# The RWKV recurrence of a three-mixer block: per-chunk state matrices in closed form, on quarters of the TensorE array

## The chip, the cores and the metric

The kernel runs on one core of one Trainium2 chip. The metric is the device time of one execution in microseconds; the kernel before takes 1756.44 us, the median of 3 runs (1751.82 to 1756.74). All views below are of one profiled execution.

## The reference

One layer of a trunk of 512 tokens and width 1024, in float32: an RMS norm, one input projection for three token mixers (RWKV-7, HGRN2, Mamba-2) and their gates, a gated sum of the three, an output projection, then a SwiGLU block of width 2816 and a final norm. The change is in the RWKV-7 mixer alone, 16 heads of width 64. Cut to its core, it computes for each head, token by token,

```
def step(state, inp):
    r_t, w_t, k_t, v_t, ka_t, kb_t = inp
    sa = jnp.einsum('bhvk,bhk->bhv', state, ka_t)
    state = (state * w_t[:, :, None, :] + sa[..., None] * kb_t[:, :, None, :]
             + v_t[..., None] * k_t[:, :, None, :])
    return state, jnp.einsum('bhvk,bhk->bhv', state, r_t)

xs = ... (r, jnp.exp(log_w), k, v, -kk, kk * a)
_, o = lax.scan(step, state0, xs)
```

followed by a norm of o over each head, a bonus term, and a gate. The state is 64x64 a head, and the recurrence runs over all 512 tokens.

## The kernel before

The two heads of a pair lie on partitions 0 to 63 and 64 to 127; there are eight pairs. The 512 tokens are cut into 8 chunks of 64. Three functions do a pair:

- `r_stage1` projects k, r and v with dense matmuls, forms the decays, the decayed queries AR (two blocks of 64 a chunk: A for the state's own correction, R for the output) and keys BK (B and K), then the masked score matrices of each chunk, SB and KAo (128 stationary columns, 64 rows, 128 moving columns, one matmul a head and chunk), and the transposes of BK and v, which give BKt and UV. UV holds, per chunk and head, the state on one half of the partitions and v on the other.
- `r_inverse` inverts the triangular part of the scores of all chunks (VectorE, and two trips through DRAM) and writes it into SB.
- `r_chain` walks through the 8 chunks in order. For each chunk: a matmul of [A scores; A] with UV (tile rw), copied to rb by ScalarE; the output's first part (tile ru, from UV); the inverse times rb (ru<-rb,SB), copied by VectorE over v in UV and by ScalarE to ub; the state's update (ru<-UV,BKt), which VectorE joins with the decayed old state (tile sx, decay WL) and writes as the state of the next chunk; the output's second part (ru<-ub,SB), copied to Ot by ScalarE. So every chunk waits for the one before it. Norm, transposes of Ot, gate and store follow.

All these small matmuls are plain f32, which the hardware runs as two passes, so each of them stands twice in the trace. The dense projections are split in a high and a low part of a faster type, three matmuls each (names hh, hl with wh, wl and the like), of 128x128 stationary and 512 or 256 moving columns.

The order of all instructions is worked out ahead of time: a recorder takes every operation with its operands, and `flush` lists them by simulated readiness and by a priority (`nc.prio`). The chain and the inverse of a pair have priority 0, stage 1 of the next pair 1, HGRN2 2, Mamba-2 3 and up; so the dense work of later stages fills TensorE's queue between the steps of a chain. TensorE takes its queue in that order. The planner's cost of a matmul is in `passes`; before, it knows one array with one end time (`self.pe`), and gives 0.02 us to a small f32 matmul whose output begins at a partition other than 0.

PSUM tiles that matter here are the single banks rd (`psk`), rs (`pss`), rw (`psr`) and ru (`psu`). Every instruction goes through one helper, so all rows carry its line L392 and are told apart by the names of tiles.

Of the kernel before, what the change touches and what calls it, by code (L numbers as in the profile page):

```python
# [14 lines left out]
AF = mybir.ActivationFunctionType  # L15
# [69 lines left out]
class Recorder:  # L85
# [6 lines left out]
    def __init__(self, tc):  # L92
# [13 lines left out]
        self.pe = (0.0, 0.0)  # L106
# [93 lines left out]
    def passes(self, out, method, args):  # L200

        n = 1
        for d in out.shape[1:]:
            n *= d
        load = args[1].shape[-1] / 1200
        if method == "transpose" or args[1].dtype == F32R:
            return load, [n / (1200 if method == "transpose" else 2226)]
        if out.offset & 0xffffff and self.region(out)[1]:
            return load, [0.02]
        return load, [n / 1200] * 2  # L210
# [31 lines left out]
    def add(self, eng, method, args, kw):  # L242
# [44 lines left out]
        for ap in wr:  # L287
# [5 lines left out]
              self.shares(eng, method, args, kw, out)]  # L293
# [4 lines left out]
    def flush(self):  # L298
# [33 lines left out]
        while left > len(order):  # L332
# [27 lines left out]
            if e == "tensor":  # L360
                load, ps = op[9]
                loaded, end = self.pe
                loaded = max(loaded, ready[k])
                for d in ps:
                    loaded = max(loaded + load, end + 0.003)
                    end = loaded + d
                self.pe = (loaded, end)
                op[4] = end - t
            t = max(t, ready[k])
            if e != "gate" and op[10]:  # L370
# [30 lines left out]
class Kern:  # L401
# [46 lines left out]
    def load_consts(self, rk):  # L448
# [6 lines left out]
        nc.sync.dma_start(out=self.m4, in_=self.cdram[:, C_M4:C_M4 + 4])  # L455
        self.one = self.t(self.mx, [P, 1], "one")
# [314 lines left out]

    def r_stage1(self, rk, p):
# [64 lines left out]

        bk = t([P, 8, 2, 64], "BK")
        halves = (slice(0, 64), slice(64, 128))
# [8 lines left out]
        for i, hs in enumerate(halves):  # L848
            nc.vector.tensor_tensor(out=bk[hs, :, 1 - i, :], in0=v3(a)[hs], in1=v3(Ei)[hs], op=ALU.mult)
# [12 lines left out]
        kao = t([P, 8, 128], "KAo", 2)  # L862
        nc.scalar.copy(out=kao[64:128], in_=arf[64:128])
        ka = (arf, kao)
# [24 lines left out]
        for g in range(2):  # L889
            pt = self.pss([P, 4, 2, 64])  # L890
            for c in range(4):
                nc.tensor.transpose(pt[:, c].rearrange("p h v -> p (h v)"), bkf[:, g * 4 + c, :], self.ident)
            nc.scalar.copy(out=bkt[:, :, g * 4:g * 4 + 4, :].rearrange("p h c v -> p c h v"), in_=pt)

        UV = t([P, 8, 2, 64], "UV", 2)
        pv = self.pss([P, 4, 2, 64])
        for c in range(NT):
            nc.tensor.transpose(pv[:, c].rearrange("p h v -> p (h v)"), v[:, c * P:(c + 1) * P], self.ident)
        for hh in range(2):
            hs = slice(hh * 64, hh * 64 + 64)  # L900
            ks = slice(64 - hh * 64, 128 - hh * 64)
            u4 = UV[:, :, hh, :].rearrange("p (c two) v -> p c two v", two=2)
            nc.scalar.copy(out=u4[ks, :, 0, :], in_=pv[0:64, :, hh, :])
            nc.scalar.copy(out=u4[ks, :, 1, :], in_=pv[64:128, :, hh, :])
            nc.gpsimd.memset(UV[hs, 0, hh, :], 0.0)
        return dict(WL=WL, KA=ka, SB=sb, BKt=bkt, UV=UV, bv=bv, dP=dP, dQ=dQ, p=p)

# [62 lines left out]
    def r_chain(self, rk, c_):  # L970
        nc = self.nc
        t = lambda shape, tag, bufs=1, dt=F32: self.t(rk, shape, tag, dt, bufs)
        KA, SB, UV, BKt, WL, p = c_["KA"], c_["SB"], c_["UV"], c_["BKt"], c_["WL"], c_["p"]
# [12 lines left out]
        Ot = t([P, 4, 2, 64], "Ot")  # L986
        sx = t([P, 64], "sx")
        H = (slice(0, 64), slice(64, 128))
        for c in range(8):
            RB, UB = self.rb, self.ub  # L990
            bw = self.psr([P, 2, 64])
            for hh in range(2):
                nc.tensor.matmul(bw[0:64, hh, :], KA[hh][:, c, 0:64], UV[:, c, hh, :],
                                 start=(hh == 0), stop=(hh == 1), skip_group_check=True)
            bu = self.psu([P, 4, 64])
            for hh in range(2):
                nc.tensor.matmul(bu[64:128, hh, :], KA[hh][:, c, 64:128], UV[:, c, hh, :],
                                 start=(hh == 0), stop=False, skip_group_check=True)
# [627 lines left out]
```

## Time and profile before

| | |
|---|---|
| median of 3 runs | 1756.44 us |
| the profiled execution | 1759.52 us |
| its span, first to last instruction | 1757.7 us |
| mean granted TensorE clock | 0.978 |
| TensorE matmul busy | 1702.4 us (97%), 10382 instructions |
| VectorE busy | 1092.3 us (62%), 2622 |
| ScalarE busy | 927.3 us (53%), 1843 |
| GpSimd busy | 261.2 us (15%), 295 |
| DMA engines' mean share | 38% |

A matmul's time in a row is from its start to its modelled end; matmuls overlap, so the distance between starts tells what each one takes. The RWKV pairs run from about 95 to 845 us, with HGRN2 and part of the Mamba-2 work between their steps. In the rows, `d`, `g`, `rd`, `m` and so on are PSUM tiles that are written, and the names behind the arrow are moving and stationary operands; 128*64 is rows by columns of the stationary operand, 128x512 partitions by moving columns.

### The profile page before, as it was taken

The page shows a single profiled execution, that of the slowest core. Times are in us where ns is not written, and L with a number is a line of the kernel's source. Part 1 is how long each engine was busy: PE and PEld are TensorE (multiplying, and loading weights), DVE is VectorE, ACT ScalarE, POOL GpSimd, SP SyncE. Part 2 cuts the span into 40 slices and gives each one's busy share as a digit, 9 for nine tenths or more (in the row PEclk, how much of TensorE's full clock was granted, in tenths as well). Part 3 has the DMA queues.
Part 4 walks back from the last instruction along what each step waited for, and adds up shares of the span by engine and source line. Part 5 has one row for each costly group of instructions (what it writes and reads, how often), then busy time and mean ns, then how long its engine had stood idle before and what let it go on. Part 6 is the DMA issues. An engine that isn't in the chain of part 4 may idle for free. (4 is left out here: it accounts for less than half of the span.)

```text
span 1757.7 us, 29033 instructions
## 1 busy us (share of the span) xinstructions
PE 1702.4 (97%) x10382; PEld 1328.1 (76%) x10382; DVE 1092.3 (62%) x2622; ACT 927.3 (53%) x1843; POOL 261.2 (15%) x295
## 2 busy tenths in 40 slices
PE   7999999999999999989999999999999999999998
PEld 6786777667676867665878978976788888888886
DVE  5778888687776888885575777554354533333233
ACT  6567665675665566665674668443343533333222
POOL 1112213131221212120120231121111000000000
PEclk9999999899997999998999999999999999999999
DMA  5242323323332233333343445377764333333222
GB/s 162 67 108 72 82 71 90 82 64 88 79 96 64 68 86 84 88 87 82 88 120 93 121 149 173 115 238 236 233 204 148 90 93 93 97 94 92 96 97 78
DMA packets 291311, 191.89 MB, mean 109 GB/s; under 512 B 59053, under 2 KB 255047, under 8 KB 291167
## 3 DMA queue, kind: packets, MB, share of 16 engines
q1 hardware_dynamic: 291167, 190.04, 37.8%
q8 instruction: 82, 1.34, 0.3%
q14 instruction: 62, 0.51, 0.1%
HBM read 164.22 MB, written 25.76 MB: 108 GB/s over the span
## 5 line engine op out<-in xcount | busy, mean ns | idle before, releaser
L392 DVE TENSOR_TENSOR wl<-wr,wh 128x512 fp32r<-128x512 f32 x267 | 187.0, 702 | 251.7 <-ACT wh L392 248.3
L392 ACT CAST wh<-wr 128x512 fp32r<-128x512 f32 x267 | 164.8, 619 | 316.4 <-PE d L392 87.4
L392 ACT CAST rgh<-rgr 128x512 fp32r<-128x512 f32 x142 | 87.8, 618 | 184.2 <-PE rd L392 84.4
L392 DVE TENSOR_TENSOR rgl<-rgr,rgh 128x512 fp32r<-128x512 f32 x142 | 100.7, 710 | 115.6 <-ACT rgh L392 112.1
L392 PE MATMUL d<-hh,wh 128*128 128x512 f32 (+1 forms) x368 | 153.8, 418 | 4.4 <-DVE q L392 3.1
L389 ACT ACT_TABLE_LOAD x121 | 155.2, 1283 | 2.1
L392 PE MATMUL d<-hl,wh 128*128 128x512 f32 (+1 forms) x368 | 152.2, 414 | 0.0
L392 PE MATMUL d<-hh,wl 128*128 128x512 f32 (+1 forms) x368 | 151.0, 410 | 0.7 <-DVE wl L392 0.7
L392 PE MATMUL rd<-hh,rgh 128*128 128x512 f32 (+1 forms) x324 | 131.0, 404 | 1.3 <-DVE r L392 0.5
L392 PE MATMUL rd<-hl,rgh 128*128 128x512 f32 (+1 forms) x324 | 128.4, 396 | 0.0
L392 PE MATMUL rd<-hh,rgl 128*128 128x512 f32 (+1 forms) x324 | 128.4, 396 | 0.0
L392 PEld LDWEIGHTS d<-hh,wh 128*128 128x128 f32 x368 | 71.9, 195 | 24.3 <-issue 6.7
L392 PE MATMUL g<-hh,gwh 128*128 128x512 f32 x192 | 82.4, 429 | 2.9 <-ACT gwr L392 1.8
L392 PE MATMUL g<-hh,gwl 128*128 128x512 f32 x192 | 81.0, 422 | 3.3 <-DVE gwl L392 3.2
L392 PEld LDWEIGHTS d<-hh,wl 128*128 128x128 f32 x368 | 71.6, 195 | 15.9 <-issue 2.2
L392 PEld LDWEIGHTS d<-hl,wh 128*128 128x128 f32 x368 | 71.7, 195 | 15.5 <-issue 2.0
L392 PE MATMUL g<-hl,gwh 128*128 128x512 f32 x192 | 80.8, 421 | 0.0
L392 PE MATMUL d<-wh,hh 128*128 128x256 f32 x256 | 74.3, 290 | 2.5 <-ACT q L392 2.3
L392 PEld LDWEIGHTS rd<-hh,rgh 128*128 128x128 f32 x324 | 61.1, 189 | 19.8 <-DVE r L392 2.3
L392 PE MATMUL d<-wl,hh 128*128 128x256 f32 x256 | 74.5, 291 | 0.0
L392 POOL TENSOR_TENSOR X<-X,q 128x256 f32<-128x256 f32 x56 | 52.3, 941 | 143.6 <-ACT X L392 133.2
L392 PE MATMUL d<-wh,hl 128*128 128x256 f32 x256 | 72.9, 285 | 0.0
(1490 smaller groups left out, 4427.1 us busy)
## 6 DMA issues: line engine op xcount, KB each, us to landing
wr<-in_w_in_dram SPq DMA_DIRECT2D x108, 256.0 KB
rgr<-in_w_in_dram SPq DMA_DIRECT2D x88, 256.0 KB
wr<-in_w_branch_dram SPq DMA_DIRECT2D x59, 256.0 KB
wr<-in_w_ffn_in_dram SPq DMA_DIRECT2D x58, 256.0 KB
gwr<-in_w_in_dram SPq DMA_DIRECT2D x96, 128.0 KB
rgr<-in_w_ffn_in_dram SPq DMA_DIRECT2D x30, 256.0 KB
wr<-in_w_ffn_out_dram SPq DMA_DIRECT2D x30, 256.0 KB
gdram<-gwr SPq DMA_DIRECT2D x24, 256.0 KB
```

The source lines that it names most:

```text
L389: self.nc.scalar.preload_act_table_set(ops[-1 - j][7])
L392: getattr(getattr(self.nc, eng), method)(*[self.resolve(x) for x in args], **{k: self.resolve(x) for k, x in kw.items()})
```

## The change

`r_chain` no longer walks the chunks with all their steps. With the state S at the head of a chunk, a chunk's new state is a matrix M times S plus a matrix N, and its output a matrix Q times S plus a local part; M, N, Q and the local part don't depend on S. They are formed for all chunks in batches (`quads` calls over c = 0 to 7), one read from PSUM a batch; then six serial steps S <- M S + N follow, and one batch adds Q S to all outputs. The decay enters M as eye times WL, made by GpSimd into AR's first half.

`quads` multiplies the two heads as two 64x64 matmuls, each on a quarter of the array (`x` = 0: rows and columns of the same half; `x` = 1: crossed halves). Many batches alternate x and the PSUM bank with the chunk's parity.

In `r_stage1`, BK is built at full height instead of in halves, the scores use quads, masked by 4 operations of 128 partitions instead of 8 of 64, and the transposes of A, v, B and K are quads against an identity of 64 (`eye`) instead of 12 transposes of 128x128; KAo's copy and the parts of UV go. The planner models each quarter of the array in 32x32 parts with their own load and end times (`self.pe`, 16 of them), at least 0.006 us between matmul starts, drops the 0.02 us rule, and counts up to 0.11 us between two operations of VectorE or ScalarE on different partitions.

```diff
+    def quads(self, out, st, mv, x=0, start=True):
+        H = (slice(0, 64), slice(64, 128))
+        for i in range(2):
+            self.nc.tensor.matmul(out[H[i ^ x]], st[H[i]], mv[H[i]], start=start, stop=True, skip_group_check=True)

 r_stage1:
-        for i, hs in enumerate(halves):
-            nc.vector.tensor_tensor(out=bk[hs, :, i, :], in0=v3(kk)[hs], in1=v3(ae)[hs], op=ALU.mult)
+        nc.vector.tensor_tensor(out=bk[:, :, 0, :], in0=v3(kk), in1=v3(ae), op=ALU.mult)
...
-        for g in range(2):
-            gs = slice(g * 4, g * 4 + 4)
-            ps = (self.psk([P, 4, 128]), self.pss([P, 4, 128]))
-            for c4 in range(4):
-                c = g * 4 + c4
-                nc.tensor.matmul(ps[1][:, c4, :], bkf[H[1], c, :], ka[1][H[1], c, :], start=True, stop=True)
-                nc.linked(nc.tensor.matmul, ps[0][:, c4, :], bkf[H[0], c, :], ka[0][H[0], c, :], start=True, stop=True)
-            for hh in (1, 0):
-                hs, ks = H[hh], H[1 - hh]
-                nc.vector.tensor_tensor(out=sb[hs, gs, :], in0=ps[hh][hs], in1=mask[hs], op=ALU.mult)
-                nc.vector.tensor_tensor(out=ka[hh][ks, gs, :], in0=ps[hh][ks], in1=mask[ks], op=ALU.mult)
+        for i, dst in enumerate((sb, ks)):
+            ps = (self.psk([P, 4, 128]), self.pss([P, 4, 128]))
+            for c in range(8):
+                self.quads(ps[c % 2][:, c // 2], bk[:, c, i], arf[:, c], c % 2)
+            for x in range(2):
+                nc.vector.tensor_tensor(out=dst[:, x::2, :], in0=ps[x], in1=mask, op=ALU.mult)
...
+        av = t([P, 2, 8, 64], "UV", 2)
+        for dst, src in ((av, (lambda c: ar[:, c, 0], lambda c: v[:, c * 64:c * 64 + 64])),
+                         (bkt, (lambda c: bk[:, c, 0], lambda c: bk[:, c, 1]))):
+            ps = (self.psk([P, 2, 4, 64]), self.pss([P, 2, 4, 64]))
+            for i in range(2):
+                for c in range(8):
+                    self.quads(ps[c % 2][:, i, c // 2], src[i](c), self.eye, c % 2)
+            for x in range(2):
+                nc.scalar.copy(out=dst[:, :, x::2, :], in_=ps[x])
+        nc.gpsimd.tensor_tensor(out=ar[:, :, 0, :], in0=self.eye.unsqueeze(1).broadcast_to([P, 8, 64]),
+                                in1=WL.unsqueeze(2).broadcast_to([P, 8, 64]), op=ALU.mult)

 r_chain, in place of the loop over the chunks:
+        At, V, B, K = AV[:, 0], AV[:, 1], BKt[:, 0], BKt[:, 1]
+        TA, SBo, Ot = SB[:, :, 0:64], SB[:, :, 64:128], t([P, 8, 64], "Ot")
+        b = self.psr([P, 8, 64])
+        for c in range(8):
+            quads(b[:, c], KS[:, c, 0:64], V[:, c])
+        nc.scalar.copy(out=Ot, in_=b)
+        ba, bv = self.psu([P, 8, 64]), self.psr([P, 8, 64])
+        for c in range(1, 8):
+            quads(ba[:, c], TA[:, c], At[:, c])
+        for c in range(8):
+            quads(bv[:, c], TA[:, c], Ot[:, c])
+        nc.vector.tensor_copy(out=TA[:, 1:8], in_=ba[:, 1:8])
+        nc.scalar.copy(out=Ot, in_=bv)
+        b = (self.psu([P, 4, 2, 64]), self.psr([P, 4, 2, 64]))
+        for c in range(1, 8):
+            quads(b[c % 2][:, c // 2, 0], TA[:, c], B[:, c], c % 2)
+            quads(b[c % 2][:, c // 2, 1], TA[:, c], SBo[:, c], c % 2)
+        for x in range(2):
+            s = AR[:, 2 - x::2]
+            nc.vector.tensor_tensor(out=s, in0=b[x][:, 1 - x:4], in1=s, op=ALU.add)
+        b = (self.psu([P, 4, 64]), self.psr([P, 4, 64]))
+        for c in range(7):
+            quads(b[c % 2][:, c // 2], K[:, c], V[:, c], c % 2, c < 2)
+        for c in range(7):
+            quads(b[c % 2][:, c // 2], B[:, c], Ot[:, c], c % 2, False)
+        for x in range(2):
+            nc.scalar.copy(out=At[:, x:7:2], in_=b[x][:, 0:4 - x])
+        b = self.psu([P, 8, 64])
+        for c in range(8):
+            quads(b[:, c], KS[:, c, 64:128], V[:, c], 0, c == 0)
+        for c in range(8):
+            quads(b[:, c], SBo[:, c], Ot[:, c], 0, False)
+        nc.scalar.copy(out=Ot, in_=b)
+        b = self.psr([P, 8, 64])
+        for c in range(1, 7):
+            quads(b[:, c], AR[:, c, 0], At[:, c - 1])
+            nc.vector.tensor_tensor(out=At[:, c], in0=b[:, c], in1=At[:, c], op=ALU.add)
+        b = (self.psu([P, 4, 64]), self.psr([P, 4, 64]))
+        for c in range(1, 8):
+            quads(b[c % 2][:, c // 2], AR[:, c, 1], At[:, c - 1], c % 2)
+        for x in range(2):
+            o = Ot[:, 2 - x::2]
+            nc.vector.tensor_tensor(out=o, in0=b[x][:, 1 - x:4], in1=o, op=ALU.add)
...
-        po = self.pss()
-        for c in range(NT):
-            nc.tensor.transpose(po[:, c * P:(c + 1) * P], Ot[:, c].rearrange("p h v -> p (h v)"), self.ident)
+        po = (self.pss([P, 4, 64]), self.psu([P, 4, 64]))
+        for c in range(8):
+            quads(po[c % 2][:, c // 2], Ot[:, c], self.eye, c % 2)

 the planner (flush):
-                load, ps = op[9]
-                loaded, end = self.pe
-                loaded = max(loaded, ready[k])
+                load, ps, parts = op[9]
+                loaded = max([ready[k]] + [self.pe[i][j][0] for i, j in parts])
+                end = max(self.pe[i][j][1] for i, j in parts)
                 for d in ps:
-                    loaded = max(loaded + load, end + 0.003)
+                    loaded = self.pe_last = max(loaded + load, end + 0.003, self.pe_last + 0.006)
                     end = loaded + d
...
+            if e in ("vector", "scalar"):
+                if self.parts.get(e) not in (None, op[11]) and t - self.free[e] < 0.1:
+                    t = max(t, self.free[e] + 0.11)
+                self.parts[e] = op[11]
```

## Rows read from the trace of the kernel before

**Rows 1.** Windows: stretch, length, busy of PE, PEld, DVE, ACT, POOL, clock, DMA.
```profile
95.00:845.00 750.00, 726.19 (x5515) 526.29 (x5516) 585.62 (x1718) 464.13 (x1029) 144.52 (x161) 0.96 0.31 80
845.00:1757.00 912.00, 897.82 (x4465) 737.39 (x4463) 444.66 (x760) 404.76 (x711) 101.67 (x106) 0.99 0.43 132
1400.00:1500.00 100.00, 100.00 (x430) 80.68 (x429) 36.95 (x55) 32.25 (x54) 0.00 (x0) 1.00 0.34 97
```

**Rows 2.** Waits of TensorE, 95 to 845: waiter, releaser, total us, times, longest.
```profile
PE ru L392 <- DVE UV L392: 1.4, 2, 0.9
```

**Rows 3.** Timeline of TensorE, one chunk of the chain: start us, us, instruction.
```profile
717.38 0.40 PE L392 MATMUL d<-hh,wh 128*128 128x512 f32 x1
717.70 0.34 PE L392 MATMUL ru<-UV,BKt 128*64 128x64 f32 x4
717.97 0.50 PE L392 MATMUL d<-hl,wh 128*128 128x512 f32 x1
718.31 0.40 PE L392 MATMUL d<-hh,wl 128*128 128x512 f32 x1
718.54 0.40 PE L392 MATMUL d<-hh,wh 128*128 128x512 f32 x1
718.87 0.33 PE L392 MATMUL rw<-UV,AR 128*64 128x64 f32 x2
...
719.46 0.40 PE L392 MATMUL ru<-ub,SB 128*64 128x128 f32 x2
...
720.13 0.39 PE L392 MATMUL d<-hh,wl 128*128 128x512 f32 x1
720.36 0.40 PE L392 MATMUL g<-hh,gwh 128*128 128x512 f32 x1
720.69 0.27 PE L392 MATMUL ru<-UV,AR 128*64 128x64 f32 x1
...
721.40 0.40 PE L392 MATMUL g<-hh,gwl 128*128 128x512 f32 x1
```

**Rows 4.** The same timeline, first and last dense start of another chunk.
```profile
141.38 0.40 PE L392 MATMUL d<-hl,wh 128*128 128x512 f32 x1
...
147.28 0.39 PE L392 MATMUL g<-hh,gwh 128*128 128x512 f32 x1
```

**Rows 5.** The same timeline, the scores of four chunks in stage 1.
```profile
78.40 0.39 PE L392 MATMUL d<-hh,wh 128*128 128x512 f32 x1
...
78.94 0.27 PE L392 MATMUL rs<-KAo,BK 64*128 64x128 f32 x1
78.95 0.27 PE L392 MATMUL rd<-AR,BK 64*128 64x128 f32 x1
79.05 0.27 PE L392 MATMUL rs<-KAo,BK 64*128 64x128 f32 x1
...
79.82 0.50 PE L392 MATMUL d<-hl,wh 128*128 128x512 f32 x1
80.16 0.40 PE L392 MATMUL d<-hh,wl 128*128 128x512 f32 x1
```

**Rows 6.** The same timeline, a batch of four transposes and the next dense start.
```profile
87.07 0.60 PE L392 MATMUL rs<-ident,BK 128*128 128x128 f32 x4
87.42 0.48 PE L392 MATMUL g<-hh,gwh 128*128 128x512 f32 x1
```

**Rows 7.** The same timeline, matmuls of HGRN2 in four column groups.
```profile
398.96 0.70 PE L392 MATMUL m<-X 128*32 128x32 f32 x56
399.59 0.50 PE L392 MATMUL d<-hh,wh 128*128 128x512 f32 x1
```

**Rows 8.** Groups of VectorE, 95 to 845: count, busy us, mean ns, idle before.
```profile
L392 DVE SCALAR_TENSOR_TENSOR UV<-sx,WL,ru 64x64 f32<-64x64 f32 x96 | 26.8, 279 | 15.7 <-PE ru L392 13.8
```

**Rows 9.** Windows, around a fall of the granted clock.
```profile
532.40:535.80 3.40, 2.45 (x18) 1.29 (x18) 3.18 (x9) 3.33 (x6) 0.00 (x0) 1.00 0.57 164
535.80:559.70 23.90, 23.67 (x101) 15.52 (x100) 12.63 (x30) 10.38 (x28) 5.72 (x5) 0.50 0.15 36
```

More of the change, by code (lines that the diff above doesn't have):

```diff
@@ L105, in __init__ @@
         self.dma = 0.0
-        self.pe = (0.0, 0.0)
+        self.pe, self.pe_last = [[(0.0, 0.0)] * 4 for _ in range(4)], 0.0
+        self.parts = {}
         self.port = {"vector": 0.0, "gpsimd": 0.0}
@@ L206, in passes @@
         if method == "transpose" or args[1].dtype == F32R:
[L207 to L210, printed above, removed]
+            ps = [n / (1200 if method == "transpose" else 2226)]
+        else:
+            ps = [n / 1200] * 2
+        rows, cols = ((q[1] // 32, -(-q[2] // 32)) for q in (self.region(args[1]), self.region(out)))
+        return load, ps, [(i, j) for i in range(*rows) for j in range(*cols)]
     def shares(self, eng, method, args, kw, out):
@@ L455, in load_consts @@
         nc.sync.dma_start(out=self.m4, in_=self.cdram[:, C_M4:C_M4 + 4])
+        self.eye = self.t(self.mx, [P, 64], "eye")
+        nc.vector.tensor_tensor(out=self.eye, in0=self.ident[:, 0:64], in1=self.ident[:, 64:128], op=ALU.add)
         self.one = self.t(self.mx, [P, 1], "one")
@@ L847, in r_stage1 @@
         nc.vector.scalar_tensor_tensor(out=a, in0=a, scalar=1.0, in1=k, op0=ALU.add, op1=ALU.mult)
-        for i, hs in enumerate(halves):
-            nc.vector.tensor_tensor(out=bk[hs, :, 1 - i, :], in0=v3(a)[hs], in1=v3(Ei)[hs], op=ALU.mult)
+        nc.vector.tensor_tensor(out=bk[:, :, 1, :], in0=v3(a), in1=v3(Ei), op=ALU.mult)
         nc.vector.scalar_tensor_tensor(out=a, in0=r, scalar=self.pc("rwkv_r_k", p), in1=a,
@@ L861, in r_stage1 @@
         arf = ar.rearrange("p c s t -> p c (s t)")
-        kao = t([P, 8, 128], "KAo", 2)
-        nc.scalar.copy(out=kao[64:128], in_=arf[64:128])
-        ka = (arf, kao)
+        ks = t([P, 8, 128], "KAo", 2)
         sb = t([P, 8, 128], "SB", 2)
@@ L888, in r_stage1 @@
         nc.gpsimd.tensor_tensor(out=bkf, in0=bkf, in1=WL.unsqueeze(2).broadcast_to([P, 8, 128]), op=ALU.mult)
[L889 to L896, printed above, removed]
-        for c in range(NT):
[L898 to L906, printed above, removed]
+        av = t([P, 2, 8, 64], "UV", 2)
[9 more added lines that the diff above has]
+                                in1=WL.unsqueeze(2).broadcast_to([P, 8, 64]), op=ALU.mult)
+        return dict(AR=ar, KS=ks, SB=sb, BKt=bkt, AV=av, bv=bv, dP=dP, dQ=dQ, p=p)
     def r_inverse(self, rk, c_):
@@ L972, in r_chain @@
         t = lambda shape, tag, bufs=1, dt=F32: self.t(rk, shape, tag, dt, bufs)
-        KA, SB, UV, BKt, WL, p = c_["KA"], c_["SB"], c_["UV"], c_["BKt"], c_["WL"], c_["p"]
+        AR, KS, SB, BKt, AV, p = (c_[i] for i in ("AR", "KS", "SB", "BKt", "AV", "p"))
         cs = slice(p * P, (p + 1) * P)
@@ L1033, in r_chain @@
+        po = (self.pss([P, 4, 64]), self.psu([P, 4, 64]))
+        for c in range(8):
+            quads(po[c % 2][:, c // 2], Ot[:, c], self.eye, c % 2)
         y = t([P, S], "y")
-        nc.vector.scalar_tensor_tensor(out=y, in0=po, scalar=self.pc("rwkv_gn_w", p), in1=c_["bv"],
-                                       op0=ALU.mult, op1=ALU.add)
+        y3, bv3 = (x.rearrange("p (c t) -> p c t", c=8) for x in (y, c_["bv"]))
+        for x in range(2):
+            nc.vector.scalar_tensor_tensor(out=y3[:, x::2], in0=po[x], scalar=self.pc("rwkv_gn_w", p),
+                                           in1=bv3[:, x::2], op0=ALU.mult, op1=ALU.add)
```

52 lines of the change are left out of this document (8 added, 44 removed).

## The prediction

> **What bounds the kernel now.** I read the busy times by stretch first. From 95 to 845 us, where the eight RWKV pairs run, TensorE is busy 726 of 750 us; behind that, 898 of 912 [rows 1]. Busy time of pipelined matmuls proves little, so the next view is the waits of TensorE in the first stretch: the longest waits for chain results come to 1.4 us in total, in a stretch of 750 [rows 2]. TensorE always has another matmul to issue, and what matters is how much of its time each piece of work takes. Then the timeline of TensorE. Undisturbed dense matmuls with 512 moving columns start every 0.2326 us (430 in 100 us) [rows 1]. Each time small f32 matmuls stand between two dense ones, the gap is longer. I price such an interruption by the time from the dense start ahead of it to the second dense start behind it, less two pitches (0.465 us); so the slow first dense matmul behind it (0.34 us to the next start) is counted.
>
> **The price of the old steps, per pair of heads.** One chunk of the old chain is in [rows 3]. The state update (ru<-UV,BKt): 718.31 - 717.38 - 0.465 = 0.465 us. The new right side with the old output (rw, then ub): 720.13 - 718.54 - 0.465 = 1.125. Output and solve (ru<-UV,AR, KAo and rb): 721.40 - 720.36 - 0.465 = 0.575. Sum 2.17 us. Another chunk took from 141.38 to 147.28, 5.90 us with 13 dense matmuls in it, so 5.90 - 13 x 0.2326 = 2.88 [rows 4]. These are my ends; I take 2.3, near the first, because in the second TensorE stood for UV. Eight chunks, the last without the update: 8 x 2.3 - 0.47 = 17.9 us. The scores: 80.16 - 78.40 - 0.465 = 1.3 per four chunks [rows 5], 2.6 for eight. The three batches of transposes in stage 1 and the one of the output: 0.35 to the next dense start [rows 6] and 0.10 for its slow start, 0.45 each, 1.8. Old total 22.3 us a pair.
>
> **The price of the new steps.** A quads call is two 64x64 matmuls of two passes each. Its passes: 128 columns are one pass per 0.11 us in a half of the array [rows 5], so 64 columns 0.055. Two row halves run at once (rs and rd start 0.01 us apart) [rows 5], and four column groups too: 56 matmuls of 32 columns in 0.63 us, 11 ns each [rows 7]. I take it that both hold together, so that the two matmuls of a call overlap, and calls on alternating banks (c % 2) use the other two quarters. No row shows row and column groups combined; from below the price is the one used here, from above every pass stands alone (a rival). Passes one behind the other, per pair: KS by V 16; TA by At 14; TA by Ot 16; TA by B and by SBo 14 calls on two banks, 16; K by V and B by Ot 16; the local outputs 2 x 16 = 32; six serial steps 12; the carried output 8; the transpose of Ot 8. That is 138 x 0.055 = 7.6 us. The fixed part of an interruption is 0.465 less its two passes, 0.35 us [rows 3]. Order and banks join some batches: I count the first two as one, then TA by Ot, TA by B, the K/B sums, the local outputs, six steps, the carried output, the transpose: 13 x 0.35 = 4.55. Chain 12.15 us. In stage 1 the scores are two groups of 8 passes of 128 columns (1.76), the transposes two groups of 16 passes (1.76), four interruptions 1.4: 4.9, where the old ones cost 3.95. New total 17.05 us.
>
> Saved: 22.3 - 17.05 = 5.25 us a pair, 42 us in eight. The issue of matmuls doesn't bind: four quarters need one per 0.055 / 4 = 14 ns, and [rows 7] has 11.
>
> The Trainium skill, TensorE: Matmul & The Clock Gate, section "Wait — 56ns, not 53.3ns?", says that matmul starts are never closer than about 25 ns, however small the matmul. The 11 ns of [rows 7] disagree for matmuls in different column groups. By the page, the 300 matmuls a pair in batches on two banks would cost 300 x 10.5 ns more, an estimate of 25 us in all; I go by the row.
>
> **What else moves.** Waits: the old chain hands over four or five times a chunk to ScalarE or VectorE and back, about 300 times in all; the new one some 13 times a pair, 104. A waiting quads call holds everything behind it on TensorE, dense matmuls included, so the six steps (quads, add of 128x64 on VectorE, quads) are the dangerous ones; dense work of later stages stands between them, as it does between the old ones. The few us of idle before chain matmuls [rows 2] fall to a third: I take -3 us, with +10 as the other end should the order written beforehand be wrong by 0.2 us at each of the 48 steps. VectorE loses 20 copies and 22 multiply-adds of 0.28 us a pair [rows 8], and as full-height instead of half-height operations 4 of the 8 score maskings and 2 of the 4 BK products; it gains about 5 us of reads from PSUM: by estimate -10 us a pair of its 586 / 8 = 73 [rows 1]. ScalarE loses about 8 us of 58. Neither bounds; they make weights ready earlier. TensorE's idle 24 us there and the gaps between dense groups shrink; I take -10 us, between 0 and -35. The extra product on GpSimd (eye by WL) costs nothing on the path: GpSimd is busy 145 of 750 us [rows 1]; uncovered it would add under 2 us a pair, ahead of the six steps. No DMA is added or moved on SP's queue. The planner's new model of TensorE and the 0.11 us it now counts for a change of partitions change the order everywhere; within +-10 us, taken as nothing.
>
> Sum: -42 - 3 - 10 = -55 us. The profiled execution took 1759.5 us (span 1757.7 and 1.8 around it): 1704.5. The median of the runs shown is 3.1 us lower, so I predict 1701 us.
>
> **Rivals.** (a) The quarters don't overlap. For: every overlapping pair of row halves in the trace writes two banks (rs and rd) [rows 5], while both matmuls of a quads call write one. If they take turns, each batch without alternation doubles (16 + 14 + 16 + 32 + 12 = 90 passes, +4.95 us) and each with it runs two at a time (48 passes, +2.64; scores +1.76; transposes +1.76): 11.1 us a pair, 89 us; 1701 + 89 = 1790. It turns the sign once more than 6.9 of these 11.1 us a pair are paid. Against: the two write different partitions, and column groups share a bank freely [rows 7]. The Trainium skill, TensorEngine Tiling (Array Packing), section "Restrictions and Gotchas", says that different row tiles cannot use the same PSUM bank at the same time; no run here shows it either way, and its time would be this 1790.
>
> (b) Two at a time but never four: only the batches on two banks suffer, 2.64 + 1.76 + 1.76 = 6.2 us a pair, 49 in all: 1750, no change or barely faster.
>
> (c) The clock. Stretches with few dense columns dropped the granted clock: 535.8 to 559.7 ran at 0.50, 1.2 GHz, after TensorE had been busy for 2.45 of 3.40 us, with 18 matmuls [rows 9]; over the 750 us the mean is 0.96 [rows 1], about 30 us lost. If each new chain brings one such stretch, 8 x 12 us = 96 less the 30 there now: 1701 + 66 = 1767. Against: the batches are shorter than the old chain and dense work lies between.
>
> (d) More is gained: half the idle (12), half the clock loss (15), and the dearer old chunk (2.88 for 2.3 in half of them, 18): about 1701 - 40 = 1660.
>
> **How the numbers follow.** Forecast 0.57 (own range 1675 to 1735), (a) 0.09, (b) 0.09, (c) 0.05, (d) 0.20. Under 0.3%, 5 us here, a measurement of this kernel can't tell a change. Faster: forecast, (d) and a third of (b), 0.80. Same: 0.07, nearly all (b). Slower: (a) most of it, and (c), 0.13. The range 1650 to 1745 holds the forecast's and most of (d), and leaves out (a), (c) and much of (b).
>
> **What would show it.** In the new trace: the two matmuls of a quads call start within 0.01 us of each other; KS by V (32 matmuls) takes about 0.9 us (1.8 would be (a)) and TA by B and SBo (56 matmuls) about 0.9 too (1.5 would be (a) or (b)); the chain breaks the dense stream some 13 times a pair, where three times a chunk is 24 now [rows 3]; the busy time of VectorE between 95 us and the end of the last pair some 80 us less; that stretch shorter by about 55 us and the rest behind it as long as now (912 us). Wrong it would be if the stretch shortened and the rest grew, or if TensorE stood for VectorE in the six steps for more than 1 us a pair.

## The result, and the profile after

The changed kernel takes 1691.07 us (median of 4 runs, 1688.76 to 1691.18); the kernel before, run beside it on the same chip, 1754.13 (4 runs, 1746.37 to 1756.74). By the medians it is 63 us faster; the ratio is 0.9662 [0.9627, 0.9697]. The profiled execution took 1688.76 us, 70.8 less than the one of before.

The totals of its page, engine by engine: busy us, share of the span, instructions.

```profile
span 1687.0 us, 34137 instructions
PE 1642.5 (97%) x13358; PEld 1331.5 (79%) x13358; DVE 1024.3 (61%) x2335; ACT 831.5 (49%) x1519; POOL 267.4 (16%) x285
```

TensorE is as full as before and has 2976 more matmuls; VectorE lost 68 us and ScalarE 96. The granted clock (span and mean) is the first difference that does not come from the arithmetic; it was 0.978 over 1757.7 us before:

```profile
core 0: 1687.0 us, clock 0.994
```

The stretches that answer to [rows 1], with the same columns. The last pair's outputs are now transposed at 690 us, not at 850. The last two stretches are explained below.

```profile
95.00:690.00 595.00, 580.59 (x7905) 465.32 (x7903) 472.81 (x1332) 333.02 (x621) 150.96 (x152) 1.00 0.34 84
690.00:1687.00 997.00, 980.44 (x4885) 801.25 (x4884) 485.61 (x842) 437.03 (x788) 100.97 (x106) 0.99 0.44 131
130.40:147.60 17.20, 16.43 (x499) 13.59 (x498) 14.44 (x33) 7.15 (x13) 3.60 (x4) 1.00 0.36 78
136.20:147.60 11.40, 11.07 (x353) 9.38 (x352) 8.99 (x24) 4.31 (x8) 3.48 (x3) 1.00 0.44 96
```

The stretch of the pairs is shorter by 155 us and the rest longer by 85: pairs now end every 77 us instead of every 94, and dense work of the other mixers that stood between them has moved behind them. So the two stretches can't be compared by themselves, only their sum. The waits of TensorE in 95 to 690 for results of the chain's steps (waiter, releaser, total us, times, longest), all that the view lists, come to 3.5 us. The row of [rows 2] is the longest of five such groups; the five come to 4.6 us in 95 to 845.

```profile
PE ru L402 <- DVE AR L402: 1.6, 2, 0.9
PE ru L402 <- ACT UV L402: 1.0, 2, 0.8
PE rw L402 <- DVE UV L402: 0.9, 2, 0.7
```

The timeline of TensorE over one chain (start us, us, instruction, matmuls in the row) answers to [rows 3]. An f32 matmul has one such record for each of its two passes, and by matmul I mean such a record, as the prediction does. KS lies in the tile named KAo, At and V in UV, B and K in BKt. The fence begins with TA by At (28 matmuls) and TA by Ot; then come parts of TA by B and by SBo on two banks, the local outputs (KS by V, then SBo by Ot), and serial steps (`rw<-UV,AR`) with the next pair's scores (`rs<-AR,BK`) between.

```profile
130.14 0.40 PE L402 MATMUL d<-hh,wl 128*128 128x512 f32 x1
...
130.66 1.03 PE L402 MATMUL ru<-UV,SB 64*64 64x64 f32 x28
131.52 0.98 PE L402 MATMUL rw<-Ot,SB 64*64 64x64 f32 x28
...
133.46 0.23 PE L402 MATMUL rw<-BKt,SB 64*64 64x64 f32 x2
133.50 0.22 PE L402 MATMUL ru<-BKt,SB 64*64 64x64 f32 x2
133.51 0.22 PE L402 MATMUL rw<-SB 64*64 64x64 f32 x2
133.56 0.22 PE L402 MATMUL ru<-BKt,SB 64*64 64x64 f32 x2
...
138.67 1.15 PE L402 MATMUL ru<-UV,KAo 64*64 64x64 f32 x32
139.66 1.04 PE L402 MATMUL ru<-Ot,SB 64*64 64x64 f32 x30
...
140.65 0.22 PE L402 MATMUL rw<-UV,AR 64*64 64x64 f32 x1
140.65 0.27 PE L402 MATMUL rs<-AR,BK 64*64 64x128 f32 x1
...
141.27 0.27 PE L402 MATMUL rw<-UV,AR 64*64 64x64 f32 x2
141.28 0.33 PE L402 MATMUL rs<-AR,BK 64*64 64x128 f32 x2
...
147.65 0.50 PE L402 MATMUL d<-hh,wh 128*128 128x512 f32 x1
```

What to see: 28 matmuls from 130.66 to 131.52 are 31 ns each in the mean. The single records behind this row start in twos: the two halves of a quads call 6 to 7 ns apart, the next two 58 ns after them. So the halves overlap in one bank. On two banks four matmuls start every 58 ns, from 133.35 to 134.3 all 56. And from 130.4 to 147.6 no projection runs, at a clock of 1.00; full-array matmuls stand there only at 134.65 and 135.80 (tmpA and tmpB by a matrix of ones, 512 columns, not in the fence), and from 136.2 on there are small ones alone.

Stage 1 of another pair, transposes of A and v (rows named `eye`), then of B and K, as the same view shows them:

```profile
224.08 0.51 PE L402 MATMUL d<-hh,wl 128*128 128x512 f32 x1
224.72 0.68 PE L402 MATMUL rd<-eye,AR 64*64 64x64 f32 x16
225.23 0.63 PE L402 MATMUL rd<-eye,v 64*64 64x64 f32 x16
225.79 0.27 PE L402 MATMUL m<-X 128*32 128x32 f32 x8
225.99 0.68 PE L402 MATMUL rs<-eye,AR 64*64 64x64 f32 x16
226.51 0.63 PE L402 MATMUL rs<-eye,v 64*64 64x64 f32 x16
...
228.63 0.50 PE L402 MATMUL g<-hh,gwh 128*128 128x512 f32 x1
```

Here all 32 matmuls of the bank rd come first and all of rs later, though the program alternates the banks call by call: the order written out beforehand takes what it reckons ready first, and rs comes free later than rd. 32 matmuls from 224.72 to 225.79 are 33.4 ns each, as if the second bank weren't there. Not every batch is split like this. By my count of the whole trace, a matmul on the other bank starts within 20 ns for 52% of the transposes of stage 1, 98% of the transposes of the outputs and 59% of TA by B and SBo, but for 14% of the K/B sums and 7% of the scores.

**Where the 70.7 us of span went.** Two sums, both from the profiled executions. First the clock: (1 - mean clock) x span is 38.7 us before and 10.1 after, a difference of 28.6; this counts the whole span as TensorE's. Second, I went through the timeline of TensorE, took each distance between two dense starts less its undisturbed pitch (doubled where the clock was low), and put it down to the small matmuls between, shared by their expected time where several kinds stand in one gap. In us, all eight pairs:

| | before | after | arithmetic alone (below) |
|---|---|---|---|
| dense matmuls at their pitch | 1284.2 | 1284.2 | 1284.2 |
| chain | 121.8 | 79.8 | 86.6 |
| scores | 32.5 | 29.2 | 29.1 |
| transposes of stage 1 | 15.0 | 39.1 | 38.0 |
| transposes of the outputs | 5.9 | 9.4 | 13.7 |
| other small matmuls | 171.6 | 168.3 | 170.3 |
| nothing between | 67.1 | 47.1 | 56.6 |
| lost by the clock | 38.7 | 10.1 | 18.9 |

The small matmuls of RWKV gave 17.7 us, gaps with nothing between 20, others 3.3, the clock 28.6: 69.6 of 70.7. How one gap is shared among kinds depends on the expected times, so these rows are estimates. A second count needs none: each small matmul gets the time to the next start, and what a dense one takes beyond its pitch goes to the small ones beside it. It gives, before and after, chain 133.0 and 80.2, scores 36.2 and 39.8, transposes of stage 1 15.2 and 29.7, transposes of the outputs 6.6 and 7.7, other small ones 202.9 and 206.6, nothing between 31.4 and 18.1, and 35.8 and 8.3 lost by the clock. Both counts agree on the chain (42 and 53 us less) and on stage 1 (21 and 18 us more); all small matmuls of RWKV together are 18 us less by the one and 34 by the other.

The clock can be checked without a model. In 44 executions of the kernel before, run beside the experiments, the mean granted clock differed from one to the next, from 0.975 (1760 to 1765 us) to 0.996 (1734.23 us); time and clock go together (correlation -0.97, 13.0 us for each 0.01). Six more executions, slow ones by over 1.5% against the fastest beside them, are not counted. The changed kernel's four executions had clocks of 0.994 to 0.997. At that clock the line through the 44 gives the old kernel some 1736 us, an estimate with one execution near it. So of the 63 us between the medians about 45 are there at the same clock, and about 18 go with the clock; the 28.6 belong to one profiled execution of before, at 0.978.

### The profile page after: what moved, and what is told of

It reads as the page before. It is cut to its first block, busy times and chain, and to the rows that moved or that the text cites. A ratio compares the mean times of both kernels' runs of the same rounds, so it can differ in the third digit from the quotient of the medians.

```text
span 1687.0 us, 34137 instructions
## 1 busy us (share of the span) xinstructions
PE 1642.5 (97%) x13358; PEld 1331.5 (79%) x13358; DVE 1024.3 (61%) x2335; ACT 831.5 (49%) x1519; POOL 267.4 (16%) x285
## 4 chain that ended last, share of the span: by engine, by line
PE 79%; DVE 7%; DMA 5%; ACT 5%; issue 2%; SPq 1%; POOL 1%; POOLq 0%; DVEq 0%; ACTq 0%
PE d L402 21%; PE rd L402 17%; PE g L402 11%; PE m L402 8%; PE rw L402 8%; PE rs L402 8%; PE ru L402 7%; DVE X L402 1%; ACT L399 1%; DMA em<-ydram 1%; DMA wr<-in_w_in_dram 1%; SPq L402 1%; DMA gwr<-in_w_in_dram 1%; DMA gdram<-gwr 1%; ACT wh L402 1%
## 5 line engine op out<-in xcount | busy, mean ns | idle before, releaser
L402 PE MATMUL d<-hh,wh 128*128 128x512 f32 (+1 forms) x368 | 148.1, 402 | 1.8 <-DVE q L402 1.2
L402 PE MATMUL d<-hh,wl 128*128 128x512 f32 (+1 forms) x368 | 147.4, 400 | 0.7 <-DVE wl L402 0.7
L402 PE MATMUL d<-hl,wh 128*128 128x512 f32 (+1 forms) x368 | 145.7, 396 | 0.0
L402 PE MATMUL g<-hh,gwh 128*128 128x512 f32 x192 | 79.8, 416 | 4.1 <-ACT gwh L402 2.0
L402 PEld LDWEIGHTS rd<-hh,rgl 128*128 128x128 f32 x324 | 61.3, 189 | 14.8 <-issue 0.7
```

The costliest lines, as they stand in the source:

```text
L402: getattr(getattr(self.nc, eng), method)(*[self.resolve(x) for x in args], **{k: self.resolve(x) for k, x in kw.items()})
```

## The experiments

The first study took the change apart into arithmetic and planner.

**planner_only**: the kernel before with the planner's part of the change.

```diff
-        self.pe = (0.0, 0.0)
+        self.pe, self.pe_last = [[(0.0, 0.0)] * 4 for _ in range(4)], 0.0
+        self.parts = {}
...
-        if out.offset & 0xffffff and self.region(out)[1]:
-            return load, [0.02]
...
+            if e in ("vector", "scalar"):
+                if self.parts.get(e) not in (None, op[11]) and t - self.free[e] < 0.1:
+                    t = max(t, self.free[e] + 0.11)
+                self.parts[e] = op[11]
```

> The arithmetic of before with the planner's new model of TensorE's quarters and of changes of partitions. If all of the gain is the arithmetic's (small matmuls cheaper, fewer waits, a clock that falls less often), the time stays within 10 us of before: 1744 to 1764 us, and the granted clock stays near 0.98. Rival: the new order is part of the gain, most of all of the clock's share; then 15 to 30 us below before, 1725 to 1740, and a clock of 0.99.

Measured: 1781.75 us (1780.31 to 1784.47), ratio to the kernel before 1.0157 [1.0115, 1.0199], slower, which neither expectation had. **math_only**: the change with the planner as before.

```diff
-        self.pe, self.pe_last = [[(0.0, 0.0)] * 4 for _ in range(4)], 0.0
-        self.parts = {}
+        self.pe = (0.0, 0.0)
...
+        if out.offset & 0xffffff and self.region(out)[1]:
+            return load, [0.02]
...
-            if e in ("vector", "scalar"):
-                if self.parts.get(e) not in (None, op[11]) and t - self.free[e] < 0.1:
-                    t = max(t, self.free[e] + 0.11)
-                self.parts[e] = op[11]
```

> The new arithmetic with the planner's old model (one array, 0.02 us for a small f32 matmul that begins at another partition than 0). If the arithmetic carries the gain: within 10 us of 1691. If the new order carries a part: 1705 to 1725.

Measured: 1719.0 us (1716.95 to 1721.03), 0.9798 [0.9754, 0.9842]. So the arithmetic alone gives 35 us (1754.4 by the ratio, less 1719.0), and the planner another 28 on top of it (to 1691), but it costs 28 where the old arithmetic stays. Span and clock of planner_only, then of math_only:

```profile
core 0: 1779.6 us, clock 0.973
```

```profile
core 0: 1717.4 us, clock 0.989
```

By (1 - clock) x span planner_only loses 48 us to the clock and math_only 18.9, where the kernel before loses 38.7 and the changed one 10.1: of each of the planner's two effects about 9 us are the clock, the rest is order at full clock.

**one_diagonal**: the matmuls of all quads use the same two quarters; the banks still alternate.

```diff
-            self.nc.tensor.matmul(out[H[i ^ x]], st[H[i]], mv[H[i]], start=start, stop=True, skip_group_check=True)
+            self.nc.tensor.matmul(out[H[i]], st[H[i]], mv[H[i]], start=start, stop=True, skip_group_check=True)
```

> As the changed kernel, but x is 0 in every quads call, so only the two quarters on the diagonal are used and no batch runs four at a time; banks, copies and counts are the same. If the alternating batches run four at a time as the prediction priced them (2.64 + 1.76 + 1.76 us a pair): +49 us, 1740. If the scores seldom do, because their two banks come free at different times: +25 to +35 us, 1716 to 1726. Rival (b) of the prediction, two at a time at most: no change, 1691 +-5.

Measured: 1711.5 us, 0.9757 [0.9708, 0.9806]: 20 us more than the changed kernel, between no change and the 25 to 35 us for banks that come free at different times; four at a time throughout was priced at 49. The timeline of TensorE in this kernel shows a part of the reason: a batch of transposes that was split by banks costs what it cost in the changed kernel.

```profile
227.33 0.68 PE L402 MATMUL rd<-eye,AR 64*64 64x64 f32 x16
227.85 0.63 PE L402 MATMUL rd<-eye,v 64*64 64x64 f32 x16
228.41 0.27 PE L402 MATMUL m<-X 128*32 128x32 f32 x8
228.61 0.68 PE L402 MATMUL rs<-eye,AR 64*64 64x64 f32 x16
```

**transposes_thrice**: each transpose of stage 1 is done three times over, 2048 more matmul records.

```diff
-            for i in range(2):
+            for i in (0, 1, 0, 1, 0, 1):
                 for c in range(8):
```

> As the changed kernel, with each batch of stage 1's transposes issued three times into the same bank: 64 more calls a pair, 256 more matmuls of 64 columns. If TensorE's time is what bounds the stretch and four quarters run at once: 2 x 1.76 us a pair, +28 us, 1719. At two at a time +56 us, 1747. If TensorE has slack there: less than +10 us.

Measured: 1765.49 us (1761.27 to 1769.96), 1.0074 [1.0047, 1.0101]: 74 us over the changed kernel, 36 ns for each added matmul, more than either expectation. This isn't the price of the matmuls alone. In the two traces the transposes of stage 1, each counted to the next start, take 26.8 us in the changed kernel and 76.2 here: 49.5 us for 2048 more, 24 ns each, between four at a time (14.4) and a split batch (33.4). The other 25 us lie elsewhere, among them longer waits of TensorE in the stretch of the pairs (for Ot and UV 6.5 and 5.9 us, against 1.8 and 0.9 in the changed kernel). So the added matmuls are on the path, and what delays them delays more.

**no_carry**: the six serial steps no longer depend on each other. Left out is the carry of the state over more than one chunk.

```diff
             quads(b[:, c], AR[:, c, 0], At[:, c - 1])
-            nc.vector.tensor_tensor(out=At[:, c], in0=b[:, c], in1=At[:, c], op=ALU.add)
+        nc.vector.tensor_tensor(out=At[:, 1:7], in0=b[:, 1:7], in1=At[:, 1:7], op=ALU.add)
```

> As the changed kernel, but the six serial steps don't wait for each other: all six multiply the uncarried states, and one add of 128x384 follows; it leaves out the carry of the state over more than one chunk. If the steps cost what the prediction gave them (five interruptions more of 0.35 us a pair): -14 us, 1677. If TensorE also stands between them: -20 to -30, 1661 to 1671. If other small matmuls fill the gaps, as the trace suggests (scores of the next pair between the steps): less than 5 us.

Measured: 1697.22 us, 0.9695 [0.9638, 0.9751]. Nothing is won, where five interruptions at the prediction's price would give 14 us. In this kernel's timeline 18 of the 24 matmuls of the steps are one batch, the other six stand among scores. The order changed elsewhere too: the view of waits now lists 4.7 us for KAo, which the changed kernel's doesn't (lines of the timeline and of the waits in 95 to 690). So a small gain from the steps may be hidden by it.

```profile
142.37 0.69 PE L402 MATMUL rw<-UV,AR 64*64 64x64 f32 x18
```

```profile
PE rd L402 <- DVE KAo L402: 4.7, 3, 2.3
```

**no_partition_rule**: the change without the 0.11 us that the planner counts between two operations on different partitions.

```diff
-            if e in ("vector", "scalar"):
-                if self.parts.get(e) not in (None, op[11]) and t - self.free[e] < 0.1:
-                    t = max(t, self.free[e] + 0.11)
-                self.parts[e] = op[11]
```

> As the changed kernel, with the planner's new model of TensorE but without its 0.11 us for a change of partitions on VectorE and ScalarE. If the model of TensorE's quarters is what made the 28 us between the old and the new planner: 1691 +-5. If the rule on partitions made it: 1710 to 1720.

Measured: 1708.14 us (1704.2 to 1711.28), 0.976 [0.972, 0.980]. With the new arithmetic, taking the rule away costs 17 of the planner's 28 us, and the new model of TensorE by itself gives the other 11. (Taken in another order the parts may differ.)

**banks_together**: the planner may begin a batch on two banks only when both are free.

```diff
+    def together(self, aps):
+        ids = [x.offset >> 24 for x in aps]
+        for i in ids:
+            self.open(i)
+            self.acc.setdefault(i, [])
+        return [self.gate[i] for i in ids if i in self.gate]
...
+            self.nc.ops[-1][5].extend(both)
...
             ps = (self.psk([P, 2, 4, 64]), self.pss([P, 2, 4, 64]))
+            both = nc.together(ps)
...
-                    self.quads(ps[c % 2][:, i, c // 2], src[i](c), self.eye, c % 2)
+                    self.quads(ps[c % 2][:, i, c // 2], src[i](c), self.eye, c % 2, both=both)
```

> As the changed kernel, but in each batch on two banks no quads call is listed before both banks are free, so that the batch isn't split into one bank after the other. In the changed kernel's trace split batches take 33.7 ns a matmul and joined ones 17. If that split is what keeps the gain below its price: -10 to -25 us, 1666 to 1681, with nearly all transposes of stage 1 near 17 ns. If waiting for both banks costs as much as it gives: 1691 +-6. Slower than 1697 if the wait delays the next pair's stage 1.

Measured: 1685.29 us (1683.39 to 1689.94), 0.9634 [0.9595, 0.9672]: 6 us under the changed kernel, with intervals that overlap: what was expected if waiting costs as much as it gives. The batches of transposes and the K/B sums did join (a matmul on the other bank within 20 ns for 89% and 86% of them, by the count above), the scores mostly not (31%). This kernel's timeline of TensorE shows the first and the last of 62 matmuls that alternate in this way:

```profile
89.89 0.22 PE L409 MATMUL rd<-eye,BK 64*64 64x64 f32 x1
89.90 0.22 PE L409 MATMUL rs<-eye,BK 64*64 64x64 f32 x1
89.90 0.22 PE L409 MATMUL rd<-eye,BK 64*64 64x64 f32 x1
89.90 0.22 PE L409 MATMUL rs<-eye,BK 64*64 64x64 f32 x1
89.95 0.22 PE L409 MATMUL rd<-eye,BK 64*64 64x64 f32 x1
...
90.77 0.23 PE L409 MATMUL rd<-eye,BK 64*64 64x64 f32 x2
```

62 matmuls in 0.89 us are 14.4 ns each: four quarters at once, at the price that the prediction used. But with the banks held back, TensorE stands for chain results more than before (waits of TensorE, 95 to 690 us, in this kernel; 0.9 us in two waits in the changed one):

```profile
PE rw L409 <- DVE UV L409: 7.4, 16, 1.6
```

The last study asked whether the planner's gain is a better model or a lucky order: **rule_008** and **rule_014** put 0.08 and 0.14 us in the rule's place, **wait_022** an unrelated latency by 0.01 us, **changed_again** nothing, and **rule_old_math** puts the rule alone into the kernel before.

```diff
 rule_008 (rule_014 has 0.14):
-                    t = max(t, self.free[e] + 0.11)
+                    t = max(t, self.free[e] + 0.08)
 wait_022:
-            return 0.21 if e == "tensor" else 0.14
+            return 0.22 if e == "tensor" else 0.14
 rule_old_math, in the kernel before:
+            if e in ("vector", "scalar"):
+                if self.parts.get(e) not in (None, op[11]) and t - self.free[e] < 0.1:
+                    t = max(t, self.free[e] + 0.11)
+                self.parts[e] = op[11]
```

> The changed kernel again, unaltered, as the yardstick for the three that follow: 1691 +-5 us.

> As the changed kernel, with 0.08 instead of 0.11 us in the planner's rule for a change of partitions. If the 17 us between the changed kernel and the one without that rule come from the rule being right (in the trace a VectorE instruction on other partitions starts 31 ns behind the end of the one before it, one on the same 128 partitions 83 ns ahead of it): within 5 us of the changed kernel, since 0.08 is nearly right. If orders that differ a little differ in time by chance: anywhere from 1680 to 1710, without relation to the rule.

> The same with 0.14. Rule right: within 5 us of the changed kernel, or a little above. By chance: anywhere from 1680 to 1710.

> As the changed kernel, with 0.22 instead of 0.21 us in the planner for the way from TensorE to another engine, which says nothing on partitions or quarters. If a good order follows from a good model: within 5 us of the changed kernel. If the order is a matter of chance: off by up to 15 us either way.

> The kernel before with the planner's rule of 0.11 us for a change of partitions, and the old model of TensorE. If the rule makes orders better because it is right: 10 to 20 us below before, 1735 to 1745, and then the new model of TensorE is what costs the old arithmetic the 31 us of planner_only. If it is the rule that harms the old arithmetic, whose chain changes partitions at nearly every step on VectorE and ScalarE: 10 to 30 us above before, 1765 to 1785.

| kernel | us (range) | ratio to before |
|---|---|---|
| changed_again | 1691.87 (1691.38 to 1695.51) | 0.9648 [0.9611, 0.9685] |
| rule_008 | 1692.68 (1688.57 to 1698.17) | 0.9652 [0.9608, 0.9696] |
| rule_014 | 1707.68 (1703.73 to 1709.95) | 0.9734 [0.9696, 0.9772] |
| wait_022 | 1688.32 (1687.55 to 1689.41) | 0.9625 [0.9589, 0.9662] |
| rule_old_math | 1809.9 (1807.29 to 1819.27) | 1.0329 [1.0285, 1.0373] |

Two small nudges, 0.08 and the other latency, moved the time by 4 us or less against changed_again, as expected if the rule is right; 0.14 moved it by 16 us, about as bad as no rule, where a right rule should have kept it within 5 or a little above. So the study leaves open whether the rule's 17 us are a better model or the chance of one order. With the old arithmetic the same rule costs 55 us, more than either expectation. The rule and the new model of TensorE together cost 28 there (planner_only), so it isn't the new model that harms the old arithmetic: it takes back about half. The windows of rule_old_math show where the time went (the stretch of the pairs; then 3.4 us ahead of one fall of the clock, and the stretch at the low level behind it):

```profile
95.00:890.00 795.00, 755.45 (x5493) 543.42 (x5492) 587.54 (x1715) 461.36 (x1026) 144.43 (x163) 0.91 0.30 76
146.50:149.90 3.40, 2.38 (x18) 1.33 (x18) 2.36 (x7) 2.92 (x8) 1.57 (x1) 1.00 0.20 77
149.90:187.40 37.50, 35.78 (x207) 22.44 (x207) 20.78 (x58) 12.29 (x40) 3.28 (x5) 0.50 0.20 47
```

And the waits of TensorE in 95 to 890 us on chain results (the longest was 1.4 us in [rows 2]):

```profile
PE ru L397 <- ACT Ot L397: 6.3, 13, 0.9
PE rw L397 <- DVE UV L397: 5.3, 11, 0.7
PE ru L397 <- DVE UV L397: 4.1, 5, 1.2
```

TensorE stands for the old chain's results more often, the clock fell to 1.2 GHz (0.50) behind such places, and (1 - 0.957) x 1809.7 = 77.8 us are lost by the clock, 39 more than before. The other 13 of the 52 us between the two profiled spans are waits and order at full clock. Why counting a price that the engines do take makes the old order worse is open; the old chain changes partitions at nearly every step of VectorE and ScalarE, so the rule moves most of its chain, but no run isolates that. The rule also counts its price where the trace shows none, between full height and the half that begins at partition 0 (last section).

## Why the prediction was right, and where its terms were off

The forecast was -55 us and the runs of one study differ by -63; in the profiled executions -70.8. The sign, the place (TensorE's own time) and the size hold. The composition doesn't: three terms were off, and the errors partly cancelled. At the same clock the change is worth about 45 us, less than the forecast; the 18 us or so of the clock, which the sum left out, made up for that. So the closeness of the number is in part luck.

**The price of the old and new matmuls (-42 forecast, -18 or -34 by the two counts).** The chain itself came near: forecast 17.9 to 11.4 us a pair (12.15 less the 0.79 of the output's transposes), measured 15.2 or 16.6 to 10.0; so the 2.3 us a chunk was too dear, and rival (d), which priced half of the chunks higher still, was wrong in that part (its three parts also add up to 45, not 40). The step that failed is stage 1: old scores and transposes were forecast at 3.95 us a pair and took 5.9 or 6.4, the new ones at 4.9 and took 8.5 or 8.7. "The scores are two groups of 8 passes" and "the transposes two groups of 16 passes" assumed that calls on two banks interleave throughout. The banks come free at different times, and nearly all batches of scores and about half of the transposes are done bank by bank, for the transposes 33.4 ns a matmul where 14.4 were possible. one_diagonal agrees (without the second diagonal 20 us are lost, not 49), since a split batch loses nothing with it. banks_together joined most batches, though not the scores, and won only 6 us: TensorE then stood 7.4 us for UV, and what the rest went into is open. So the split is shown, but not that it is all of the miss in stage 1.

**The order ("within +-10 us, taken as nothing").** This was the largest miss in kind. The planner's new model is worth -28 us with the new arithmetic and +28 with the old one. The four corners, medians: old with old 1754, old arithmetic with the new planner 1782, new with the old planner 1719, new with new 1691. Neither part has a value of its own here: the arithmetic is worth 35 us under the one planner and 91 under the other. A forecast that adds parts one by one can't see that; the prediction should have kept a wider end for the order.

**The clock (taken as unchanged, half of its loss given back in rival (d)).** 28.6 of the 70.7 us of the profiled pair, and about 18 of the 63 between the medians, go with the clock. The premise of (c), that each new chain brings a fall, is refuted: between 95 and 690 us the changed kernel's clock fell once, for 3.4 us, and in the stretches above it stayed at 1.00, with TensorE busy 16.43 of 17.20 us and, among small matmuls alone, 11.07 of 11.40. In the kernel before it fell six times between 95 and 845 us, 58 us in all. Three of the falls, 41 us, stand behind steps of a chain: [rows 9], and those at 331.0 and 832.7. The windows of before ahead of these two:

```profile
327.60:331.00 3.40, 1.85 (x17) 0.93 (x15) 3.31 (x7) 3.22 (x7) 0.00 (x0) 1.00 0.53 159
829.30:832.70 3.40, 2.20 (x13) 1.25 (x13) 3.12 (x9) 2.90 (x8) 0.00 (x0) 1.00 0.52 156
```

The other three follow waits for Ot (the normed output of a pair, 1.3 us), for a weight (gwr, 1.8) and for q (3.1). So in these rows TensorE stood still ahead of the falls, mostly between old steps, and the lack of dense columns alone went with no fall. That the missing waits are what gave the clock back is the reading of these rows; no run changed the waits alone.

**Waits and relief (-3 and -10 forecast).** The waits listed for chain results fell from 4.6 to 3.5 us, not to a third. Gaps with nothing between fell by 13 or 20 us by the two counts, the 13 of both terms together or somewhat more. VectorE lost 68 us over the span, against about 80 (10 a pair). The six steps were, as far as the runs show, priced too high: no_carry, in which they don't wait, doesn't give back the 14 us of five interruptions, and the +10 end wasn't needed. The timeline shows the next pair's scores and other small matmuls between the steps (140.65 to 141.28 above). The sign against itself that the prediction named, more than 1 us a pair of standing for VectorE in the steps, didn't come: 0.9 us in all pairs.

**The marks.** The two matmuls of a call start 6 to 7 ns apart, within the 0.01 us named; 32 of them from 138.67 to 139.66 take 0.99 us (0.9 forecast, 1.8 for rival (a)); TA by B and SBo, 56 matmuls, about 0.95 us (0.9; 1.5 for (a) or (b)). Both rivals' mechanisms are refuted: two and four at a time both occur. A part of (b)'s price was paid all the same, by the split of banks. The chain breaks the dense stream 5 to 6 times a pair, not 13, by my count, against 27 before: many batches follow one another or have only other small matmuls between. The mark on the stretches was wrong: the one shrank by 155 us and the rest grew by 85, which the prediction had named as a sign against itself. It was no sign against the mechanism: the pairs just ran closer together.

**The two rules.** Rows first: 28 matmuls from 130.66 to 131.52 us, two row halves in one bank, start in twos, 6 to 7 ns apart, with 58 ns from one two to the next; the two write different partitions of the bank. The Trainium skill, TensorEngine Tiling (Array Packing), "Restrictions and Gotchas", says that different row tiles can't access the same PSUM bank at the same time; this trace disagrees where the partitions differ, and the measurement decides. And 62 matmuls in 0.89 us are 14.4 ns from start to start, where the page TensorE: Matmul & The Clock Gate of the Trainium skill, "Wait — 56ns, not 53.3ns?", gives about 25 ns as the least; across quarters of the array this trace goes below it.

**What is still open.** Whether the 17 us with no rule and the 16 us with 0.14 are the model or chance; why the rule harms the old arithmetic; where most of the gain of joined banks went. wait_022 and banks_together are 3 and 6 us under the changed kernel; the intervals of their ratios overlap with its own, and they were not combined.

## What to carry to other kernels

When a written-out order depends on a cost model, a change of the model is a change of the kernel: try model and arithmetic alone and together, since their effects don't add. Where two matmuls shall use the array side by side on two banks, look in the timeline whether they do; a bank that comes free later splits the batch, here at 33.4 ns a matmul instead of 14.4. And sum the granted clock over the span before explaining a difference by matmuls; better still, look for executions of the two kernels at the same clock.

## What the runs showed of the hardware

Two operations one behind the other on VectorE overlap when their first partition is the same and the second doesn't wait for what the first wrote. They don't overlap when the first partition is another one. The timeline of VectorE of the kernel before shows both within 3 us. In the order of the program the first product of BK is on the half from partition 0, the second on the half from partition 64; the products of AR have full height:

```profile
67.46 0.68 DVE L392 SCALAR_TENSOR_TENSOR AR<-kk,E 128x512 f32<-128x512 f32 x1
68.06 0.68 DVE L392 TENSOR_TENSOR BK<-kk,tmpA 64x512 f32<-64x512 f32 x1
68.67 0.68 DVE L392 TENSOR_TENSOR AR<-r,E 128x512 f32<-128x512 f32 x1
69.38 0.69 DVE L392 TENSOR_TENSOR BK<-kk,tmpA 64x512 f32<-64x512 f32 x1
```

Full height and the first half start 0.60 and 0.61 us apart, though each takes 0.68: the next begins 82 and 73 ns before the end of the last. The second half begins 32 ns after it. The maskings of the scores agree: SB behind KAo, both on the half from 0, begins 72 to 76 ns before the end (12 of 12 times); AR on the half from 64 behind SB on the half from 0 begins 13 to 32 ns after it (12 of 12). Two halves one behind the other take 1.39 us in the same kernel (two operations of full height take 1.28 in the kernel after, wl<-wr,wh at 133.86):

```profile
143.50 1.39 DVE L392 TENSOR_TENSOR BK<-kk,tmpA 64x512 f32<-64x512 f32 x2
```

Over the trace of before, by my count of operations that begin less than 60 ns after the last one's end, in the median: with 128 partitions in both and no such wait the next begins 83 ns before the end (VectorE, 1370 times; ScalarE 95 ns, 566 times). Where one of the two has fewer, it begins 31 ns after it (188 times; ScalarE 24 ns, 153 times), but a quarter of these on VectorE overlap. And 128 partitions that wait for what the last one wrote begin 34 ns after it (166 times). The difference between the first two, 0.11 to 0.12 us, is the planner's 0.11; the rule counts it for any change of the partitions, also from full height to the first half, where the rows show none. A full-height operation in place of two halves saves more than the second one's time.

The granted clock stayed at 2.4 GHz (1.00) through 11.4 us of small f32 matmuls alone, with TensorE busy 11.07 us of them. Two quarters that write one bank took their passes side by side, and the four quarters together took a 64x64 pass every 14.4 ns.
